# Spreading the expert gates of the first 128 tokens over the units of the U loop, from the unit at which they are known

## The chip, the cores and the metric

One core of a Trainium2 chip runs the whole program. The metric is the device time of one execution in microseconds (us), as the median of several runs. A TensorE product here is one matmul instruction with its weight load. Engines are named as the profile names them: PE is TensorE, DVE is VectorE, ACT is ScalarE, POOL is GpSimd.

## The reference, cut to what matters

The program is four layers on 256 tokens of width 1024. Two of them end in a block of many small experts (`peer`), the part that is changed. For each token eight heads each choose 16 of 16,384 experts, and the block sums over the chosen ones:

```
s = einsum('thpk,hpnk->thpn', q, sub_keys)          # two times 128 scores for each head
sv, si = top_k(s, 16)                               # level 1: the best 16 of each 128
cand = sv[:, :, 0, :, None] + sv[:, :, 1, None, :]  # level 2: the best 16 of the sums
fv, fpos = top_k(cand, 16);  gate = softmax(fv)
act = gelu(einsum('thkd,td->thk', u[eidx], x_t))
return einsum('thk,thkd->td', gate * act, v[eidx])
```

## The kernel before, in words

The kernel gathers nothing. It computes the products of all 16,384 rows of `u` with all 256 tokens, multiplies by a dense matrix of gates (zero where an expert was not chosen), and multiplies the result with all rows of `v`. So each `peer` layer has a **U loop** and a **V loop** of 128 **units** each; one unit is 128 experts. `peer` runs twice; the two are called the first and the second layer here.

One unit of the U loop takes these steps:
- a DMA brings 128 rows of `u` into a `raw` buffer (SP's queue);
- DVE transposes them in blocks, `uT` (L231), one unit further ahead than the next step;
- ACT rounds `uT` to the upper part `hi` (L159, the line of all ACT work);
- POOL forms the rest `lo = uT - hi` in four pieces of 256 columns (L261). `hi` and `lo` have two buffers each;
- PE makes 24 products (L2039): eight of `hi` with the tokens' upper part, eight of `hi` with their lower part, and, in the third pass, eight of `lo`;
- ACT applies the gelu, and the 128 x 256 result goes to the unit's slot in SBUF (`slots` for units 0 to 95, `slotb` for 96 to 127).

**Choosing the experts** goes on beside the units, as generators in `self.bgs`. `tick(1300)` (L2055) lets them go on by a fixed planned time per unit. `level1` and `level2` are almost all DVE work. They work on one half of the tokens (128) at a time, and at the end of each `level2` the count `state["have"]` goes up by 64 pairs of tokens (L1933). In the order of instructions this is at unit 29 for the first half and at unit 59 for the second.

**The gates** are made from that for two tokens at a time; there are NH = 128 such pairs, and one pair is called a gate below. `gate_ab` (L1942, DVE) marks the chosen second indices in `B`. `gates_words` (ACT, two instructions) scales by the weights into `A`. `gate_mm` (L1964, PE, four products of 128 columns) forms the gates of the pair in PSUM. For each two gates (four tokens) `gate_out` writes the result to the slots: where a unit has its gelu already, DVE multiplies the slot by the gate (L1978); where it has not, ACT copies the gate into the slot. From then on `gelu` multiplies the first `n` columns of each later unit by the gates in its slot (L2006, DVE), with a second ACT instruction for them.

Each engine runs its instructions in the order written. Within unit i that is: `gate_out` of gates whose products were made in unit i-1, `take()` (the next `hi`, `lo` and a transpose), the words of the marks made in unit i-1, the 24 products of unit i with the gate products between the second and third pass, the gelu of unit i-1, the planned share of the choosing, and last the marks `B` of the next gates. How many marks that are is what `due` says, lines L2057 to L2060.

Of the kernel before, what the change touches and what calls it, by code (L numbers as in the profile page):

```python
# [38 lines left out]
P = 128  # L39
# [78 lines left out]
class _Kernel:  # L118
# [1587 lines left out]
    def peer(self, l, after=None, result=None):  # L1706
        nc, a, T = self.nc, self.a, NX
        tc = self.tc
        with ExitStack() as st:
# [43 lines left out]
            with ExitStack() as s2:  # L1753
# [181 lines left out]
                NH = T // 2  # L1935
                ab, gps = {}, {}
                todo = {"ab": 0, "words": 0, "mm": 0, "out": 0}
# [9 lines left out]
                def gates_words():  # L1947

                    for g in range(todo["words"], todo["ab"]):
                        A = pu.tile([P, 2, P], F32, name=self.uid("A"), tag="A", bufs=4)  # L1950
                        for i in range(2):
                            self.act(A[:, i, :], ab[g][0][:, :, 0, i], "Copy", scale=gW[:, 2 * g + i:2 * g + i + 1])
                        ab[g] += (A.bitcast(F16).rearrange("p i (k n) -> p i n k", n=2),)
                    todo["words"] = todo["ab"]
# [27 lines left out]
                def gates_out():  # L1982
                    while todo["out"] * 2 + 2 <= todo["mm"]:
                        gate_out(todo["out"])
                        todo["out"] += 1

                def gates_mm(upto):
                    while todo["mm"] < upto:
                        gate_mm(todo["mm"])
                        todo["mm"] += 1  # L1990

                def gates_ab(n):
                    while n > 0 and todo["ab"] < NH:
                        gate_ab(todo["ab"])
                        todo["ab"] += 1
                        n -= 1

                def gelu(i, ps):
                    n = state["g"]
                    sl = slot(i)  # L2000
                    if n:
                        self.act(ps[:, :n], ps[:, :n], "Gelu")
                    if n < T:
                        self.act(sl[:, n:], ps[:, n:T], "Gelu")
                    if n:
                        nc.vector.tensor_mul(sl[:, :n], sl[:, :n], ps[:, :n])  # L2006
                    state["u"] = i + 1
# [20 lines left out]
                due = 0.0  # L2028
                for i in range(P):
                    gates_out()  # L2030
                    hi, lo = self.take()
                    gates = todo["words"]
                    gates_words()
                    ps = self.bank("mm")
                    for pas, (w, x) in enumerate(((hi, hh), (hi, hl), (lo, hh))):
                        if pas == 2:
                            gates_mm(gates)
                        for c in range(KC):
                            nc.tensor.matmul(ps[:, :T], w[:, c * P:(c + 1) * P], x[:, c, :],  # L2039
                                             start=(pas == 0 and c == 0), stop=(pas == 2 and c == KC - 1))  # L2040
                    if self.pend or self.follow or self.hooks:
                        self.after_unit(0.0)
                        assert i < 8
                    elif not slotb:
                        pq.close()
                        bigb = st.enter_context(tc.tile_pool(name=f"slotsb{l}", bufs=1))
                        slotb.append(bigb.tile([P, (P - NA) * NX], F32, name=f"slotb{l}"))
                    if prev is not None:
                        gelu(i - 1, prev)
                    prev = ps  # L2050
                    if i == 59:
                        assert not self.bgs
                    have = state["have"]
                    if self.bgs:
                        self.tick(1300)  # L2055
                    if have:
                        due = min(due + min((NH - todo["ab"]) / max(P - 3 - i, 1.0), 9.0 if have == NH else 0.01), 2.0)  # L2057
                        n = min(int(due), have - todo["ab"])
                        gates_ab(n)
                        due -= n  # L2060
# [224 lines left out]
```

## Time and profile before

| | us |
|---|---|
| median of 3 runs (2311.14 to 2314.92) | 2312.92 |
| the profiled execution | 2311.26 |
| its span, first to last instruction | 2309.5 |
| U loop of the first layer, span 512.56 to 941.46 | 428.90 |
| U loop of the second layer, span 1515.12 to 1943.16 | 428.04 |

The span is counted from the first instruction, and all positions below are microseconds from there. Stretches of the U loop are cut at the first of PE's 24 products of a unit. In the first layer unit 28 starts at 607.92, unit 32 at 619.36, unit 40 at 643.61, unit 44 at 657.74, unit 48 at 673.69, unit 52 at 687.07, unit 56 at 701.54, unit 60 at 713.10, unit 72 at 752.31 and unit 76 at 765.83.

How to read it: an engine that is busy for the whole of a stretch sets the pace there. Where none is, the pace is set by a chain of waits from one engine to the next.

### The profile page before, as it was taken

The page shows a single profiled execution, that of the slowest core. Times are in us where ns is not written, and L with a number is a line of the kernel's source. Part 1 is how long each engine was busy: PE and PEld are TensorE (multiplying, and loading weights), DVE is VectorE, ACT ScalarE, POOL GpSimd, SP SyncE. Part 2 cuts the span into 40 slices and gives each one's busy share as a digit, 9 for nine tenths or more (in the row PEclk, how much of TensorE's full clock was granted, in tenths as well). Part 3 has the DMA queues.
Part 4 walks back from the last instruction along what each step waited for, and adds up shares of the span by engine and source line. Part 5 has one row for each costly group of instructions (what it writes and reads, how often), then busy time and mean ns, then how long its engine had stood idle before and what let it go on. Part 6 is the DMA issues. An engine that isn't in the chain of part 4 may idle for free. (4 is left out here: it accounts for less than half of the span.)

```text
span 2309.5 us, 42025 instructions
## 1 busy us (share of the span) xinstructions
PE 2186.9 (95%) x14729; PEld 1964.3 (85%) x14729; DVE 1764.0 (76%) x3502; ACT 1291.2 (56%) x2608; POOL 1730.9 (75%) x2070
## 2 busy tenths in 40 slices
PE   8988997898999999999999988998999999999997
PEld 7768886898989999887787877998899999888886
DVE  5938888578787999678979776796969997555555
ACT  2435664554437888544444645554458886545454
POOL 1107978788999888876666685579999888777775
PEclk9999999999999999999999989999999999999999
DMA  5327755477878777577888532687878786555554
GB/s 164 110 82 235 238 172 189 134 193 149 172 154 168 156 157 155 174 254 278 306 295 306 171 110 92 195 168 150 165 159 163 156 156 155 196 196 183 200 187 141
DMA packets 285582, 414.88 MB, mean 180 GB/s; under 512 B 16489, under 2 KB 217386, under 8 KB 285370
## 3 DMA queue, kind: packets, MB, share of 16 engines
q1 hardware_dynamic: 279722, 405.30, 64.2%
q10 hardware_dynamic: 5648, 6.89, 1.1%
q8 instruction: 116, 1.90, 0.4%
q14 instruction: 96, 0.79, 0.1%
HBM read 408.98 MB, written 3.15 MB: 178 GB/s over the span
## 5 line engine op out<-in xcount | busy, mean ns | idle before, releaser
L261 POOL TENSOR_TENSOR lo<-raw,hi 128x256 fp32r<-128x256 f32 x956 | 874.9, 944 | 380.1 <-ACT hi L159 369.5
L261 POOL TENSOR_TENSOR lo<-uT,hi 128x256 fp32r<-128x256 f32 x1022 | 779.8, 801 | 80.0 <-ACT hi L159 79.5
L159 ACT ACTIVATE hi<-raw 128x1024 fp32r<-128x1024 f32 x380 | 400.7, 1057 | 422.2 <-DMA raw<-in_peer_v 200.1
L2039 PE MATMUL mm<-h,hi 128*128 128x256 f32 x4096 | 530.9, 282 | 18.8 <-ACT hi L159 17.5
L2039 PEld LDWEIGHTS mm<-h,hi 128*128 128x128 f32 x4096 | 504.4, 189 | 23.1 <-ACT hi L159 20.3
L263 DVE TENSOR_TENSOR lo<-raw,hi 128x512 fp32r<-128x512 f32 (+1 forms) x290 | 224.6, 775 | 237.1 <-ACT hi L159 236.0
L231 DVE STREAM_TRANSPOSE uT<-raw 128x1024 f32<-128x1024 f32 x256 | 316.5, 1236 | 105.1 <-POOL lo L261 78.7
L159 ACT ACTIVATE hi<-uT 128x1024 fp32r<-128x1024 f32 x256 | 271.2, 1059 | 212.0 <-DVE uT L231 196.6
L2039 PE MATMUL mm<-h,lo 128*128 128x256 f32 x2048 | 312.1, 290 | 14.2 <-POOL lo L261 11.5
L2039 PEld LDWEIGHTS mm<-h,lo 128*128 128x128 f32 x2048 | 263.8, 189 | 27.0 <-POOL lo L261 26.6
L2090 PE MATMUL mm<-hi,whi 128*128 128x512 f32 x1024 | 277.4, 392 | 4.0 <-ACT hi L159 3.6
L2090 PE MATMUL mm<-lo,whi 128*128 128x512 f32 x1024 | 275.5, 390 | 0.8 <-POOL lo L261 0.8
L2090 PE MATMUL mm<-hi,wlo 128*128 128x512 f32 x1024 | 274.7, 390 | 1.5 <-DVE wlo L494 1.5
L2090 PEld LDWEIGHTS mm<-hi,whi 128*128 128x128 f32 x1024 | 190.8, 188 | 48.0 <-ACT hi L159 6.9
L2090 PEld LDWEIGHTS mm<-lo,whi 128*128 128x128 f32 x1024 | 191.4, 188 | 43.7 <-POOL lo L261 4.2
L2090 PEld LDWEIGHTS mm<-hi,wlo 128*128 128x128 f32 x1024 | 191.9, 188 | 42.7 <-DVE wlo L494 2.7
L406 PE MATMUL mm<-h,hi 128*128 128x258 f32 (+2 forms) x1344 | 207.1, 297 | 19.8 <-ACT h L159 8.9
L406 PEld LDWEIGHTS mm<-h,hi 128*128 128x128 f32 x1344 | 181.9, 197 | 26.0 <-ACT h L159 9.9
L1942 DVE TENSOR_TENSOR B<-sin,ij 128x512 f16<-128x512 bf16 x256 | 182.8, 751 | 0.0
L159 ACT ACTIVATE A<-B,cos 128x128 f32<-128x128 f16 x512 | 167.9, 403 | 0.0
L494 DVE TENSOR_TENSOR wlo<-slots,whi 128x256 fp32r<-128x256 f32 x192 | 158.1, 824 | 0.6
L406 PE MATMUL mm<-h,lo 128*128 128x258 f32 (+2 forms) x672 | 108.8, 295 | 3.7 <-POOL lo L261 3.1
(480 smaller groups left out, 2763.7 us busy)
## 6 DMA issues: line engine op xcount, KB each, us to landing
raw<-in_peer_u SPq DMA_DIRECT2D x512, 256.0 KB
raw<-in_peer_v SPq DMA_DIRECT2D x128, 1024.0 KB
slots<-in_ada_w SPq DMA_DIRECT2D x56, 512.0 KB
scratch<-in_ada_w SPq DMA_DIRECT2D x40, 512.0 KB
raw<-in_sb_w_in SPq DMA_DIRECT2D x32, 512.0 KB
raw<-in_peer_w_q SPq DMA_DIRECT2D x32, 512.0 KB
raw<-in_od_w_in SPq DMA_DIRECT2D x24, 512.0 KB
raw<-in_ab_w_in SPq DMA_DIRECT2D x22, 512.0 KB
```

What stands on the lines that cost most here:

```text
L159: self.nc.scalar.activation(out=out, in_=in_, func=getattr(ACTF, func), **kw)
L231: self.nc.vector.transpose(ut.rearrange("p b c e -> p c b e"), src)
L261: nc.gpsimd.tensor_sub(lo[:, sl], src[:, sl], hi[:, sl].bitcast(F32))
L263: nc.vector.tensor_sub(lo[:, n:], src[:, n:], hi[:, n:].bitcast(F32))
L406: nc.tensor.matmul(ps[mm][:, :T], w[:, o:o + P], x[:, j * 4 + kk, :T], start=(j == 0 and n_of[mm] == 1), stop=(j == nu - 1 and n_of[mm] == ...
L494: nc.vector.tensor_sub(lo, src, hi.bitcast(F32))
L1942: nc.vector.tensor_tensor(out=B.rearrange("p j n i -> p j (n i)"), in0=iota4, in1=ij[:, g].rearrange("p n i -> p (n i)").unsqueeze(1).to_b ...
L2039: nc.tensor.matmul(ps[:, :T], w[:, c * P:(c + 1) * P], x[:, c, :], start=(pas == 0 and c == 0), stop=(pas == 2 and c == KC - 1))
L2090: nc.tensor.matmul(outs[t][d], w[:, t * P:(t + 1) * P], v[:, 512 * d:512 * d + 512], start=(i == 0 and pas == 0), stop=(i == P - 1 and pas ...
```

## The change

One line is changed. `due` is the number of gates owed; each unit adds to it the gates left to make, over the units left up to three before the end.

```diff
                     if have:
-                        due = min(due + min((NH - todo["ab"]) / max(P - 3 - i, 1.0), 9.0 if have == NH else 0.01), 2.0)
+                        due = min(due + (NH - todo["ab"]) / max(P - 3 - i, 1.0), 2.0)
                         n = min(int(due), have - todo["ab"])
                         gates_ab(n)
                         due -= n
```

Before, the added amount was held to 0.01 while only the first half of the tokens was known, so the first mark stood at unit 59, and from unit 67 on each unit made two. Now marks stand from unit 29 on, in the pattern 1, 1, 2. The total stays at 128 gates in each layer. Whatever stands behind a gate moves with it: two ACT words, four PE products, and the write to the slots. Since gates now come earlier, more of `gate_out` is ACT copies and less DVE products, and more units have gated columns in their gelu.

DVE, unit 41 of the first layer, from where the choosing for the second half of the tokens goes on (`slots` holds its scores and indices) to the transpose of unit 42. Before:

```order
L1738 MATCH_REPLACE slots_4220<-slots_4220 128x54 x2
L1741 MAX slots_4220<-slots_4220 128x8 x2
L1744 MAX_INDEX slots_4220<-slots_4220 128x8 x2
L1875 COPY slots_4220<-slots_4220 128x8
L1876 TENSOR_TENSOR slots_4220<-slots_4220 128x8x15
L1877 CAST slots_4220<-slots_4220 128x128
L1882 TENSOR_SCALAR slots_4220<-slots_4220 128x128 x8
L1884 TENSOR_SCALAR slots_4220<-slots_4220 128x128
L231 STREAM_TRANSPOSE uT_6863<-raw_70 128x4x8x32
```

The same place now:

```order
L2006 TENSOR_TENSOR slots_4220<-slots_4220,mm_6919 128x24
L1738 MATCH_REPLACE slots_4220<-slots_4220 128x54 x2
L1741 MAX slots_4220<-slots_4220 128x8 x2
L1744 MAX_INDEX slots_4220<-slots_4220 128x8 x2
L1875 COPY slots_4220<-slots_4220 128x8
L1876 TENSOR_TENSOR slots_4220<-slots_4220 128x8x15
L1877 CAST slots_4220<-slots_4220 128x128
L1882 TENSOR_SCALAR slots_4220<-slots_4220 128x128 x8
L1884 TENSOR_SCALAR slots_4220<-slots_4220 128x128
L1942 TENSOR_TENSOR B_7031<-sin_90,ij 128x512
L1978 SCALAR_TENSOR_TENSOR slots_4220<-aux_6936,slots_4220 128x41x4
L231 STREAM_TRANSPOSE uT_7047<-raw_70 128x4x8x32
```

The choosing stands at the same unit as before; the transpose now stands behind a gelu's product, a mark and a `gate_out` product as well (in every third unit two marks and no `gate_out`). From unit 29 to unit 58, 40 marks, 18 `gate_out` products (of 128 to 228 columns) and 26 gelu products (of 4 to 72 columns) are added on DVE in this way; 16, 8 and 11 of them in units 32 to 43. A mark of unit i has its products on PE in unit i+2, so 38 gates have theirs before unit 60.

ACT, late in the U loop of the first layer, one unit and the start of the next (`A` are the words of a gate; each has four products on PE). Before:

```order
L159 ACTIVATE hi_10059<-uT_10007 128x1024
L159 ACTIVATE A_10072<-B_10052,cos_89 128x128 x2
L159 ACTIVATE A_10075<-B_10054,cos_89 128x128 x2
L159 ACTIVATE mm_10015<-mm_10015 128x156
L159 ACTIVATE slotb_5212<-mm_10015 128x100
L159 ACTIVATE slotb_5212<-s_10095 128x26x4
L159 ACTIVATE hi_10122<-uT_10070 128x1024
```

Now, where as many tokens have their gates:

```order
L159 ACTIVATE hi_9648<-uT_9603 128x1024
L159 ACTIVATE A_9661<-B_9643,cos_89 128x128 x2
L159 ACTIVATE mm_9611<-mm_9611 128x156
L159 ACTIVATE slots_4220<-mm_9611 128x100
L159 ACTIVATE slots_4220<-s_9681 128x6x4
L159 ACTIVATE slotb_5212<-s_9681 128x32x4
L159 ACTIVATE hi_9706<-uT_9659 128x1024
```

In place of two gates in each late unit there is one in two units of three and two in the third.

## Rows read from the trace of the kernel before

**Rows 1.** Page, part 1: busy us (share of the span) x instructions
```profile
span 2309.5 us, 42025 instructions
PE 2186.9 (95%) x14729; PEld 1964.3 (85%) x14729; DVE 1764.0 (76%) x3502; ACT 1291.2 (56%) x2608; POOL 1730.9 (75%) x2070
```
**Rows 2.** Stretches, first layer: units 28-31, 32-39, 40-43, 44-47, 48-51, 52-55, 56-59, 28-59
```profile
core 0: us, PE busy (x) PEld busy (x) DVE busy (x) ACT busy (x) POOL busy (x), PEclk, DMA share, GB/s
607.92:619.36 11.44, 11.44 (x99) 11.44 (x98) 10.00 (x39) 5.33 (x8) 11.13 (x16) 1.00 0.98 187
619.36:643.61 24.25, 23.75 (x195) 22.99 (x194) 22.45 (x94) 10.65 (x16) 22.28 (x33) 1.00 0.86 169
643.61:657.74 14.13, 11.67 (x99) 11.37 (x97) 13.50 (x64) 5.13 (x8) 10.83 (x16) 0.99 0.83 171
657.74:673.69 15.95, 14.43 (x97) 13.19 (x98) 11.37 (x11) 5.53 (x9) 15.95 (x17) 0.90 0.67 133
673.69:687.07 13.38, 12.37 (x99) 11.55 (x98) 8.77 (x10) 5.33 (x8) 13.38 (x17) 1.00 0.78 156
687.07:701.54 14.47, 12.56 (x99) 11.64 (x97) 9.35 (x15) 8.09 (x11) 12.31 (x17) 1.00 0.75 148
701.54:713.10 11.56, 11.56 (x102) 11.56 (x101) 6.29 (x9) 5.33 (x8) 11.49 (x18) 1.00 0.85 168
607.92:713.10 105.18, 97.77 (x775) 93.75 (x774) 81.74 (x235) 45.38 (x67) 97.36 (x129) 0.98 0.81 161
```
**Rows 3.** Waits of DVE in units 28-39, then in units 44-55
```profile
DVE uT L231 <- DMA raw<-in_peer_u: 2.5, 2, 1.3
...
DVE uT L231 <- POOL lo L261: 14.2, 11, 3.1
```
**Rows 4.** Groups of ACT, units 28-59: busy, mean ns | idle before, releasers
```profile
L159 ACT ACTIVATE hi<-uT 128x1024 fp32r<-128x1024 f32 x32 | 33.9, 1060 | 56.5 <-DVE uT L231 54.4 <-DVE slots L1732 2.1
```
**Rows 5.** Stretches, first layer: units 72-75, 112-115, 60-127
```profile
752.31:765.83 13.52, 13.52 (x130) 13.36 (x130) 12.95 (x21) 12.03 (x37) 12.30 (x17) 1.00 0.76 157
887.78:901.35 13.57, 13.57 (x130) 13.41 (x129) 13.57 (x25) 11.30 (x33) 12.13 (x17) 1.00 0.80 156
713.10:941.46 228.36, 228.36 (x2146) 225.71 (x2145) 212.34 (x356) 192.29 (x555) 207.94 (x276) 1.00 0.78 159
```
**Rows 6.** Gate products on PE (L1964 alone), units 72-75
```profile
752.31:765.83 13.52, 2.66 (x32) 2.02 (x32) 1.00 0.76 157
```
**Rows 7.** The marks, line L1942: duration ns min/median/max
```profile
L1942 DVE TENSOR_TENSOR B<-sin,ij x256: 376/690/972, 713.5 to 1932.9; 128x512 f16<-128x512 bf16 x128
```
**Rows 8.** The marks alone, units 60-71
```profile
713.10:752.31 39.21, 13.36 (x22) 1.00 0.84 168
```
**Rows 9.** Groups by shape on DVE, units 60-127
```profile
L1978 DVE SCALAR_TENSOR_TENSOR slots<-aux,slots 128x244 f32<-128x244 f32 x1 | 0.4, 396 | 0.0
L1978 DVE SCALAR_TENSOR_TENSOR slotb<-s,slotb 128x120 f32<-128x120 f32 x1 | 0.3, 272 | 0.0
L2006 DVE TENSOR_TENSOR slots<-slots,mm 128x68 f32<-128x68 f32 x1 | 0.2, 224 | 0.2 <-ACT slots L159 0.2
L2006 DVE TENSOR_TENSOR slots<-slots,mm 128x4 f32<-128x4 f32 x2 | 0.2, 119 | 0.0
```
**Rows 10.** Stretches, second layer: units 28-59, 32-43, 60-127
```profile
1610.23:1714.52 104.29, 96.31 (x774) 92.21 (x773) 82.28 (x235) 45.37 (x67) 97.14 (x129) 1.00 0.81 163
1621.62:1659.38 37.76, 34.96 (x291) 34.20 (x289) 36.27 (x157) 15.78 (x24) 33.26 (x49) 1.00 0.85 173
1714.52:1943.16 228.64, 228.64 (x2147) 225.96 (x2146) 212.30 (x356) 192.11 (x555) 207.76 (x275) 1.00 0.79 158
```
**Rows 11.** Groups of POOL, units 28-31, units 44-47, units 72-75
```profile
L261 POOL TENSOR_TENSOR lo<-uT,hi 128x256 fp32r<-128x256 f32 x16 | 11.3, 739 | 0.3 <-ACT hi L159 0.3
...
L261 POOL TENSOR_TENSOR lo<-uT,hi 128x256 fp32r<-128x256 f32 x17 | 16.2, 994 | 3.0 <-ACT hi L159 3.0
...
L261 POOL TENSOR_TENSOR lo<-uT,hi 128x256 fp32r<-128x256 f32 x17 | 13.0, 802 | 1.2 <-ACT hi L159 1.1
```
**Rows 12.** Stretches before, in and behind a fall of the granted clock
```profile
652.00:657.70 5.70, 3.25 (x27) 3.05 (x26) 5.56 (x17) 1.09 (x2) 2.70 (x4) 0.99 0.75 174
...
657.70:661.10 3.40, 3.38 (x16) 3.38 (x17) 2.55 (x3) 1.57 (x3) 3.36 (x4) 0.52 0.22 74
661.10:664.52 3.42, 3.42 (x30) 3.30 (x29) 2.44 (x2) 1.33 (x2) 3.42 (x4) 1.00 1.14 204
```

## The prediction

> **What bounds the kernel now.** I read the page's busy shares first [rows 1]: PE is busy for 95% of the span, DVE and POOL for 75 to 76%. That is an average over unlike stages, so I cut the U loop into stretches of four to eight units next. They show two regimes.
>
> Late in the loop, from unit 60 to the end, PE is busy for 228.36 of 228.36 us [rows 5]. Four units with two gates each take 13.52 us there (3.38 a unit), and 13.57 us forty units later. DVE goes from 12.95 busy to 13.57 of 13.57 between these two rows and the pace does not follow it: PE sets it. The 32 products of eight gates can be seen in the row for L1964 alone [rows 6].
>
> In the middle, units 28 to 59, no gate is made and nothing is full throughout: of 105.18 us PE is busy for 97.77, POOL for 97.36, DVE for 81.74 [rows 2]. Units 28 to 31 are PE's pace without gates, 11.44 us of 11.44, 2.86 a unit. Units 32 to 43 belong to DVE, which chooses the experts of the second half: 35.95 of 38.38 us. ACT waits 54.4 us for the transpose in units 28 to 59 [rows 4], so what delays DVE is passed to ACT, POOL and PE. In units 44 to 51 POOL is full, 29.33 of 29.33 us, and DVE has 20.14 us of work; its idle time in units 44 to 55 is a wait of 14.2 us for POOL to release buffers [rows 3].
>
> So the change takes work from a stretch that PE paces to one where DVE, POOL and PE in turn set the pace.
>
> **What is taken away: late units.** A late gate costs PE the difference of two paces: (13.52 - 11.44) us / 8 gates = 0.26 us [rows 2, 5]. By the order, 38 gates of a layer have their products before unit 60 now. From unit 60 on PE is therefore relieved of 38 x 0.26 = 9.9 us a layer. The next engine there leaves room: with 1.33 gates a unit DVE loses a third of its marks, POOL has 12.30 of 13.52 us, ACT 12.03 [rows 5], and PE's new pace is 2.86 + 1.33 x 0.26 = 3.21 us a unit, 12.83 for four. I take the whole 9.9 us.
>
> **What is added: DVE in units 29 to 58.** A mark takes 0.376 us at its shortest and 0.972 at its longest [rows 7]; the 22 marks of units 60 to 71, where POOL is nearly full as in the middle, cover 13.36 us, 0.607 each [rows 8]. I take 0.607. A `gate_out` product of 120 columns takes 0.272 us and one of 244 takes 0.396 [rows 9], so those of 128 to 228 columns are near 0.33, and near 0.30 in units 32 to 43. A gelu product takes 0.119 us for 4 columns and 0.224 for 68 [rows 9], on average 0.155, and 0.14 in units 32 to 43. The sum is 40 x 0.607 + 18 x 0.33 + 26 x 0.155 = 24.3 + 5.9 + 4.0 = 34.2 us a layer. DVE's idle time in units 28 to 59 is 105.18 - 81.74 = 23.4 us [rows 2], so even a perfect packing leaves 10.8 us over. By stretch, for the first layer:
> - Units 32 to 43: 16 x 0.607 + 8 x 0.30 + 11 x 0.14 = 13.6 us more on DVE, into 38.38 - 35.95 = 2.4 us of idle time: +11.2 us. The four marks of units 29 to 31 (2.4 us) find 11.44 - 10.00 = 1.4 us: +1.0.
> - Units 44 to 51: 11 marks, 5 and 8 products are 9.8 us; DVE goes to 30.0 us against 29.33, and POOL grows as well. Its subtraction takes 0.739 us beside no mark and 0.802 beside two a unit [rows 11], so one mark costs POOL 4 x 0.063 / 2 = 0.13 us, 1.4 us for 11. Two engines, each full and each waiting for the other, lose more than the larger of these: I take +3, between 0.7 and the whole 9.8.
> - Units 52 to 55: 4.9 us onto 9.35 of 14.47: +0.5, for the order in which it comes.
> - Units 56 to 59: PE's own pace with gates, 12.83 against 11.56: +1.3.
>
> That is 17.0 us. In the second layer the same DVE work meets 37.76 - 36.27 = 1.5 us of idle time in units 32 to 43 in place of 2.4 [rows 10]: 17.7 us or so. Its late part is as the first layer's, 228.64 us of PE.
>
> **Edits at nothing.** The added ACT work in the middle (two words of a gate, copies, a second gelu instruction) is at most what late units do, 12.03 us in 13.52 [rows 5], where units 32 to 39 use 10.65 of 24.25 [rows 2]. If that cover were gone, `hi` would be late by the same amount. PE's added gate products, 9.9 us, fill its waits in units 32 to 55, which the terms above lengthen. No DMA and no instruction of SP's or POOL's queue is moved past another. The V loop is untouched.
>
> **Sum.** 17.0 - 9.9 = +7.1 us in the first layer and 17.7 - 9.9 = +7.8 in the second, +14.9 together. On the profiled execution's own 2311.26 us (span 2309.5) that is 2326; the median shown, 2312.92, lies 1.7 above, so I predict 2328 us.
>
> **A rule weighed.** Two engines share a way into SBUF here, and the row puts the price of a mark for POOL at 0.13 us [rows 11]. The Trainium skill, "SBUF — State Buffer", section "Who interferes with whom", says that a VectorE instruction with two SBUF inputs contends with a GpSimd instruction that reads SBUF, and that the one that starts second is blocked until the other has ended. By that rule a mark would cost POOL its whole length, not 0.13 us; the late units, with two marks each, do not show it, though the marks' own lengths, from 0.376 to 0.972 us [rows 7], agree with one engine held up by the other. What it would make of the time is the third rival.
>
> **The rivals.**
> 1. Faster: the marks only fill waits and PE's work alone counts. For it: DVE idles 23.4 us in the middle and PE 7.4. PE would then need 97.77 + 9.9 = 107.7 us for units 28 to 59 in place of 105.18, +2.5, and each layer gains 7.4: 2311 - 15 = 2296, 2298 by the median. It needs DVE's lead over PE, two units of buffers, to outlast units 32 to 43. Against it: there DVE has 13.6 us more for 2.4 us of room, and the lead is used up already where PE waits, 11.67 busy of 14.13 us in units 40 to 43 [rows 2]. It decides once the added DVE work in units 32 to 43 fits their 2.4 us of room; with the shortest marks it is still 16 x 0.376 + 3.9 = 9.9. Chance 0.08.
> 2. No change: all marks at 0.376 us. Then units 28 to 43 pay 20 x 0.376 + 3.9 - 3.9 = 7.5 us, units 56 to 59 1.3, the rest nothing, and 8.8 stands against 9.9: 2309, 2311 by the median. For it: POOL is less than full while DVE paces, and marks beside an idle POOL may be short. Against it: POOL is not idle for long, 22.28 of 24.25 us in units 32 to 39 [rows 2]. Chance 0.10.
> 3. POOL is blocked for a mark's whole length. Full POOL in units 44 to 51 then pays 11 x 0.607 = 6.7 us and not 1.4, some 5 us a layer: 2338 by the median. For it: beside the long choosing instructions of units 44 to 47 a subtraction takes 0.994 us and not 0.739 [rows 11]. Chance 0.12.
> 4. Nothing is hidden: every added DVE instruction lengthens the units, since `gate_out` and gelu products now make DVE wait for PE, where it ran ahead. 34.2 - 9.9 = 24.3 us a layer: 2361 by the median. Against it: products of the gates are two units old and DVE has shown no wait for PE in these units [rows 3]. Chance 0.06.
>
> That the change does not do what it says is excluded: the order shows the 40 marks.
>
> PE's clock can add a little to all of these. Before units 44 to 47, PE was busy for 3.25 of 5.70 us, and the granted clock then fell to 0.52 for 3.40 us, which is the level of 1.2 GHz; PE made 16 products in it and 30 in the next 3.42 us at 1.00 [rows 12]. More starving of PE may bring more such stretches, each worth up to 1.7 us; where DVE sets the pace they are hidden. I leave them out of the sum and keep them in the upper end.
>
> **How the numbers follow.** The forecast has the rest, 0.64; its own range is 2318 to 2340 (the units 44 to 51 between 0.7 and 6 us a layer, marks between 0.5 and 0.7). A measurement of this kernel can tell about 0.2%, 4.6 us, from no change, so the bounds are 2308.3 and 2317.5. Faster: rival 1 and a little of rival 2, 0.10. Within: most of rival 2 and the lower edge of the forecast, 0.10. Slower: 0.80. The range from 2311 to 2346 holds the forecast, rival 3 and half of rival 2; rivals 1 and 4 lie outside.
>
> **What would show it.** Units 32 to 43 at 49 to 51 us in place of 38, with DVE full and PE starved: if they stay under 43, the middle is wrong. Late units at 3.2 us with PE still full: if they stay at 3.38, the gain is not there, and if DVE or POOL is full in them, PE was not alone. Marks in the middle near 0.6 us. Units 44 to 51 above 31 us, and POOL's subtractions there near 1.0 us or longer. If the whole is not slower, the added DVE work must have found more idle time than 23.4 us, or have become shorter than 0.6 us a mark.

## The result and the profile after

The changed kernel takes 2330.9 us, median of 4 runs (2328.75 to 2337.51), against 2312.03 us for 4 runs of the kernel before: a ratio of 1.0097, 95% interval 1.0073 to 1.0121. It is slower, by 18.9 us by the medians; 15 were forecast. The profiled execution took 2330.08 us against 2311.26.

The page's first part, as in [rows 1], shows almost nothing of this:

```profile
span 2328.3 us, 42061 instructions
PE 2197.2 (94%) x14729; PEld 1973.4 (85%) x14729; DVE 1761.2 (76%) x3540; ACT 1312.7 (56%) x2686; POOL 1746.7 (75%) x2070
```

No share moves by more than a point, since the work is nearly the same and mostly its place is another. The stretches show it. These are, of the first layer after, units 28-31, 32-43, 44-51, 52-55, 56-59, then units 72-75, 60-127 and 28-59; the columns are those of [rows 2]:

```profile
611.45:623.32 11.87, 11.87 (x104) 11.79 (x102) 10.30 (x41) 6.05 (x10) 11.22 (x16) 1.00 0.99 190
623.32:673.60 50.28, 44.37 (x354) 41.79 (x352) 48.39 (x191) 31.42 (x83) 35.76 (x48) 0.93 0.65 129
673.60:705.13 31.53, 28.52 (x237) 26.33 (x238) 30.33 (x40) 20.91 (x56) 30.15 (x33) 1.00 0.68 134
705.13:722.16 17.03, 14.22 (x119) 13.03 (x117) 13.96 (x29) 12.97 (x32) 12.39 (x17) 1.00 0.65 126
722.16:735.35 13.19, 13.19 (x122) 13.02 (x120) 12.11 (x22) 10.75 (x30) 12.48 (x18) 1.00 0.76 157
774.15:787.23 13.08, 13.08 (x123) 12.92 (x121) 10.11 (x17) 9.92 (x29) 12.65 (x17) 1.00 0.83 164
735.35:954.92 219.57, 219.57 (x1994) 216.86 (x1993) 177.39 (x291) 165.97 (x455) 210.70 (x275) 1.00 0.80 164
611.45:735.35 123.90, 112.17 (x927) 105.96 (x925) 115.09 (x319) 82.09 (x208) 101.99 (x129) 0.97 0.70 139
```

Units 32 to 43 go from 38.38 us [rows 2, its second and third row] to 50.28, with DVE busy for 48.39. The late units go from 228.36 [rows 5] to 219.57, still PE's from end to end. The second layer repeats both; its units 28-59, 32-43, 52-55 and 60-127 answer to [rows 10]:

```profile
1620.10:1742.68 122.58, 110.97 (x927) 104.64 (x924) 115.48 (x318) 81.96 (x210) 101.60 (x128) 0.99 0.69 138
1631.86:1680.98 49.12, 43.33 (x354) 40.58 (x352) 47.25 (x191) 30.79 (x81) 34.72 (x46) 0.97 0.64 129
1712.50:1729.50 17.00, 14.20 (x118) 13.01 (x117) 13.94 (x29) 12.96 (x32) 12.38 (x17) 1.00 0.61 126
1742.68:1961.97 219.29, 219.29 (x1994) 216.56 (x1993) 178.87 (x291) 165.15 (x452) 209.97 (x275) 1.00 0.80 164
```

Units 28 to 59 lose 18.7 and 18.2 us, the late units return 8.8 and 9.4: +18.8 together, the whole difference of the two profiled executions. (The second layer's unit 28 before is taken at its first product, 1610.15; the row in [rows 10] starts 0.08 us later.) Units 0 to 27, whose order is the same, took 2.9 us longer in this profile and the rest of the program 2.9 less. Over the profiles with that order (the two kernels and experiments 1 to 4 and 9) units 0 to 27 lie between 95.0 and 97.4 us a layer, so this is the runs' own variation.

What DVE was given, units 28-59 of the first layer, in groups:

```profile
L1942 DVE TENSOR_TENSOR B<-sin,ij 128x512 f16<-128x512 bf16 x40 | 27.8, 713 | 0.0
L2006 DVE TENSOR_TENSOR slots<-slots,mm 128x8 f32<-128x8 f32 (+17 forms) x26 | 4.4, 171 | 5.1 <-ACT slots L159 4.4
L1978 DVE SCALAR_TENSOR_TENSOR slots<-s,slots 128x132 f32<-128x132 f32 (+8 forms) x9 | 3.0, 336 | 0.3 <-ACT slotb L159 0.3
L1978 DVE SCALAR_TENSOR_TENSOR slots<-aux,slots 128x128 f32<-128x128 f32 (+8 forms) x9 | 3.0, 330 | 0.3 <-ACT slotb L159 0.3
```

The busy times of these groups add up to 38.2 us, where 34.2 was forecast: the marks are longer, 27.8 us for 40, 0.69 each, where the forecast took 0.607 by the same measure. But DVE's busy time in the stretch rises only by 115.09 - 81.74 = 33.4 us. Records of neighbours on the engine overlap at their ends: all its groups here add up to 131.2 us for 115.09 busy, and before to 91.6 for 81.74, so the overlap grew with the work. The two errors cancel. And ACT's waits in the same units:

```profile
ACT A L159 <- DVE B L1942: 26.6, 28, 3.4
ACT hi L159 <- DVE uT L231: 7.8, 11, 2.4
ACT slots L159 <- DVE slots L1890: 2.8, 1, 2.8
ACT slots L159 <- DVE slots L1884: 2.7, 1, 2.7
```

Before, ACT waited 54.4 us for the transposition [rows 4]. Now it waits for marks, with `hi` queued behind its copies of them. The engine that is late is the same one.

### The profile page after: what moved, and what is told of

Same layout as the page of the kernel before. It is cut to its first block, busy times and chain, and to the rows that moved or that the text cites. A ratio compares the mean times of both kernels' runs of the same rounds, so it can differ in the third digit from the quotient of the medians.

```text
span 2328.3 us, 42061 instructions
## 1 busy us (share of the span) xinstructions
PE 2197.2 (94%) x14729; PEld 1973.4 (85%) x14729; DVE 1761.2 (76%) x3540; ACT 1312.7 (56%) x2686; POOL 1746.7 (75%) x2070
## 5 line engine op out<-in xcount | busy, mean ns | idle before, releaser
L261 POOL TENSOR_TENSOR lo<-uT,hi 128x256 fp32r<-128x256 f32 x1022 | 794.1, 814 | 86.9 <-ACT hi L159 83.3
L2039 PE MATMUL mm<-h,lo 128*128 128x256 f32 x2048 | 316.6, 293 | 12.1 <-POOL lo L261 10.3
L159 ACT ACTIVATE A<-B,cos 128x128 f32<-128x128 f16 x512 | 175.7, 402 | 53.5 <-DVE B L1942 53.5
L1942 DVE TENSOR_TENSOR B<-sin,ij 128x512 f16<-128x512 bf16 x256 | 175.2, 704 | 0.0
```

The costliest lines, as they stand in the source:

```text
L159: self.nc.scalar.activation(out=out, in_=in_, func=getattr(ACTF, func), **kw)
L261: nc.gpsimd.tensor_sub(lo[:, sl], src[:, sl], hi[:, sl].bitcast(F32))
L1942: nc.vector.tensor_tensor(out=B.rearrange("p j n i -> p j (n i)"), in0=iota4, in1=ij[:, g].rearrange("p n i -> p (n i)").unsqueeze(1).to_b ...
```

## The experiments

Pairs of values below are first layer / second layer. Runs with an interval have several rounds; the others are one profiled run, read by their stretches.

**1. Gates only from unit 44.** The changed kernel, with nothing made in the stretch that DVE paces:

```
-                    if have:
+                    if have and i >= 44:
```

> The changed kernel, but the gates of the first half are held until unit 44, so that the stretch that DVE fills (units 32 to 43) has no marks. If DVE's work there is the price: units 32 to 43 take 38 us again (50 in the changed kernel), units 44 to 59 some 6 to 8 us more than in the kernel before (23 gates), the late units 5 to 6 us less, so 0 to +2 us a layer and 2312 to 2318 us. If each gate before unit 60 costs the same wherever it stands (18.5 us for 40, 0.46 each): +11 and -5.5 a layer, 2323 us.

2314.9 us against 2310.26, ratio 1.002 (1.0001 to 1.004). Its units 32-43, 52-55 and 60-127:

```profile
620.37:658.12 37.75, 34.74 (x290) 33.94 (x288) 35.89 (x156) 15.75 (x24) 33.19 (x48) 0.99 0.87 173
688.46:706.80 18.34, 15.56 (x123) 14.66 (x121) 15.28 (x30) 13.88 (x34) 13.55 (x18) 0.91 0.64 123
720.19:943.58 223.39, 223.39 (x2062) 220.67 (x2061) 193.40 (x322) 176.10 (x497) 209.05 (x275) 1.00 0.79 161
```

Units 32-43 are back at 37.75 / 37.18 us: the 12 us a layer are paid for gates made there. But units 52-55 become 18.34 / 18.47, longer than in either kernel, and keep this version from gaining. Part of that may be PE's clock: the granted clock fell once inside these units in both layers (0.91 is the mean of the stretch), and did not in either layer of the two kernels.

**2. Marks alone.** The kernel before, with 16 marks more in units 32 to 43 that nothing reads:

```
+                    if 32 <= i < 44:
+                        for _ in range(2 if i % 3 == 1 else 1):
+                            spare_mark()
```

> The kernel before, with 16 marks that nobody reads added on DVE in units 32 to 43 of each layer; no words, no products, no writes to the slots. If DVE's time sets the pace there: 16 x 0.61 - 2.4 = 7 to 8 us more in these units (45 to 46 us in place of 38.4), nothing elsewhere, 2325 to 2328 us in all. If the price of the changed kernel comes from the gates' PE products, ACT words or copies: under 2 us in these units.

Units 32-43:

```profile
620.30:664.11 43.81, 37.99 (x290) 36.14 (x288) 43.14 (x169) 15.74 (x24) 35.22 (x47) 0.96 0.77 149
620.30:664.11 43.81, 0.00 (x0) 0.00 (x0) 7.97 (x13) 0.00 (x0) 0.96 0.77 149
```

43.81 / 43.94 us, +5.4 / +6.2 where 7 to 8 was expected: DVE is full (43.14). The second line, of the marks alone, says why it is less: only 13 of the 16 ran before unit 44 began (14 in the second layer). Their 7.97 us less the 2.4 us of idle time is 5.5, what was measured; in the second layer 8.76 less 1.5 is 7.3, for a measured 6.2. In the changed kernel 16 marks run in these units, and marks alone make about half of its +11.9. What brought the rest, the gate and gelu products (3.9 us in the forecast), the three marks more or the waits around them, no run separates.

**3. Products alone.** The kernel before, with the gates' work on PE in the middle and none of DVE's: 4 spare 128x128 products a unit (8 in every third) in units 31 to 59.

```
+                    if 31 <= i < 60:
+                        for k in range(8 if i % 3 == 0 else 4):
+                            nc.tensor.matmul(ps[:, T + k % 2 * P:T + (k % 2 + 1) * P], spare[:, :P], spare[:, :P],
```

> The kernel before, with 4 or 8 products of 128 columns added on PE at the end of each of units 31 to 59 (as many as the changed kernel has gate products there), nothing on other engines. If PE's added work hides in its waits there: units 28 to 59 take 105 to 109 us (105.2 before). If PE's time counts in full: 115 us.

Units 28-59:

```profile
612.77:719.78 107.01, 104.27 (x926) 100.73 (x925) 83.00 (x237) 46.41 (x68) 99.77 (x132) 1.00 0.83 162
```

107.01 / 106.37 us, +1.8 / +2.0, while PE's busy time grows by 6.5: PE's part is mostly hidden in its waits, as the prediction had it. Units 32-43 take 38.82 / 38.32 us of it, +0.4 / +0.6.

**4. Products put back late.** The changed kernel, with 152 spare products (38 gates' worth) in the late units that lost a gate:

```
+                    if i >= 61:
+                        for k in range(4 * lack[i]):
+                            nc.tensor.matmul(ps[:, T + k % 2 * P:T + (k % 2 + 1) * P], spare[:, :P], spare[:, :P],
```

> The changed kernel, with 4 products of 128 columns added in late units, 152 in each layer, so that PE has as much work from unit 60 on as in the kernel before; DVE, ACT and POOL keep the changed kernel's lighter load. If PE sets the pace of the late units: units 60 to 127 take 227 to 229 us (228.4 before, 219.5 in the changed kernel). If DVE's marks set it: 219 to 221 us.

Units 60-127:

```profile
729.20:959.72 230.52, 230.52 (x2147) 226.24 (x2145) 178.31 (x290) 164.61 (x450) 209.21 (x274) 1.00 0.75 156
```

230.52 / 230.54 us, a little above the 227 to 229 expected: PE's products alone take the whole gain away again, with DVE's and ACT's relief left in place. PE sets the late pace.

**5. Without the gates' exponential.** The stretch that surprised was units 52-55. There ACT loads a table, takes the exponential of the second half's gates and loads the old table again. The changed kernel with a constant in place of the exponential, so that neither load is needed (the exponential is left out):

```
-                    self.act(gt3, gt3, "Exp")
+                    self.act(gt3, gt3, "Identity", scale=0.0, bias=self.ones[:, :1])
```

> The changed kernel without the exponential of the gates: an ACT instruction that writes ones stands in its place, so the two table loads around it are gone, and its wait for DVE's last sum (L1912) stays. If units 52 to 55 are long (17.0 us in place of 14.5 before) because the gelu, and with it DVE's gelu product, waits behind the two table loads of 1.28 us each and the exponential: 14.5 to 15.5 us. If DVE's own added work is the reason: 16.5 to 17.1.

Units 52-55:

```profile
705.68:721.28 15.60, 13.59 (x118) 12.80 (x117) 14.00 (x30) 10.90 (x31) 14.78 (x17) 1.00 0.68 134
```

15.60 / 16.04 us in place of 17.03 / 17.00, between the two expectations. Without the loads these units are 1.4 / 1.0 us shorter, and DVE's longest wait for a gelu falls from 2.60 to 0.6 us. The kernel before has the same two loads, and no run takes them out there; so how much of the +2.6 / +2.8 they make is not shown.

**6. The exponential one unit later.** In the kernel before, ACT loads the table and then waits 3.46 us for the subtraction ahead of the exponential (the first two lines), with `hi` of the next unit behind it:

```profile
689.39 1.28 ACT L153 ACT_TABLE_LOAD   x1
694.13 0.31 ACT L159 ACTIVATE slots<-slots 128x128 f32<-128x128 f32 x1 [3.46 <-DVE slots L1912]
694.34 1.04 ACT L159 ACTIVATE hi<-uT 128x1024 fp32r<-128x1024 f32 x1
```

So the kernel before with the exponential issued later than the subtraction:

```
                     nc.vector.tensor_sub(gt3, fv3, fv3[:, :, 0:1].to_broadcast([P, 8, 16]))
+                    yield 1300.0
                     self.act(gt3, gt3, "Exp")
-                    yield 2000.0
+                    yield 700.0
```

> The kernel before, with the exponential written one unit later than DVE's sum that it waits for; nothing is left out. If the wait of ACT for that sum (3.5 us in units 52 to 55) holds back the upper parts behind it: units 52 to 55 take 12.3 to 13 us in place of 14.5, 1.5 to 2.2 us a layer, with a little more in units 20 to 25, 2306 us or a ratio of 0.997 to 0.9985 in all. If POOL or PE fills these units anyway: no change.

2305.01 us against 2309.45, 5 rounds, ratio 0.9977 (0.996 to 0.9994). Units 52-55 and the same instructions:

```profile
686.38:699.35 12.97, 12.37 (x98) 11.65 (x97) 10.06 (x15) 8.21 (x11) 12.58 (x17) 1.00 0.71 142
...
691.90 1.28 ACT L153 ACT_TABLE_LOAD   x1
693.69 0.31 ACT L159 ACTIVATE slots<-slots 128x128 f32<-128x128 f32 x1 [0.51 <-DVE slots L1912]
```

12.97 / 13.70 us in place of 14.47 / 14.19; the wait is 0.51. This beats both kernels, by 0.2% the one before. The two stretches are 2.0 of the 4.4 us; in units 20 to 27, where the exponential of the first half stands, this profile is 0.1 us longer and 1.2 us shorter than the one before, and where the rest comes from is open.

**7 and 8. The same edit beside the added gates:** on experiment 1, and on the changed kernel.

> First-half gates from unit 44 on as in the run from_44, and the exponential one unit later. There, units 52 to 55 took 18.4 us and units 44 to 51 30.3, against 5 us less in the late units. If the wait for the exponential is what the gates meet in units 52 to 55: these take 14 to 15.5 us, and the whole is 3 to 4 us a layer below the run from_44: 2306 us, a ratio near 0.998. If DVE's added work is: 2313 to 2315.

> The changed kernel with the exponential one unit later. The stretch that DVE fills is as in the changed kernel: units 32 to 43 stay at 49 to 51 us. If the wait for the exponential is the price in units 52 to 55: 14 to 15 us there in place of 17.0, 2323 to 2326 in all. If not: 17 us and 2330.

On experiment 1: 2310.21 us, ratio 1.0005 (0.9991 to 1.0019), units 52-55 18.23 / 20.31. On the changed kernel: 2328.9, units 52-55 16.40 / 17.17. Both missed what was expected of the wait, 14 to 15.5 and 14 to 15: with gates in these units the exponential's wait is not the main thing that makes them long. A load then stands ahead of a gelu, and DVE's gelu product waits for that, 2.5 us and 1.9 us in the first layers. The granted clock fell inside these units in both layers of the first of the two (mean 0.91 and 0.92) and in the second layer of the other (0.90); the 16.40, with no fall, is the cleanest of the four.

**9 and 10. The gelu product one unit later,** so that DVE doesn't stand at it while ACT is late: on the changed kernel, and on experiment 7.

```
+                    gated()
                     if n:
-                        nc.vector.tensor_mul(sl[:, :n], sl[:, :n], ps[:, :n])
+                        wait.append((sl[:, :n], ps[:, :n]))
```

> The changed kernel with each gelu product of DVE (L2006) written one unit later, behind the next unit's; nothing is left out, and the exponential stays where it was. If units 52 to 55 are long because DVE, in order, waits 2.6 us for a gelu that stands behind the table loads: 15 to 16 us in place of 17.0, and units 32 to 43 as they were (49 to 51). If DVE's added work alone makes them long: 16.8 to 17.3.

> First-half gates from unit 44, the exponential one unit later, and the gelu product one unit later. With the wait for the gelu gone from DVE: units 52 to 55 at 14.5 to 16 us (18.2 to 20.3 without the last step), units 56 to 59 at 13.4 and the late units 5 us below the kernel before: 2302 to 2306 us, ratio 0.996 to 0.998. If the marks themselves fill these units: 18 us there, and 2310 us, ratio 1.000.

On the changed kernel 2320.76 us in one run: units 32-43 48.77 / 48.49, 44-51 30.81 / 30.84, but units 52-55 still 17.24 / 17.37. DVE's wait there has only moved, to the gate product:

```profile
DVE slots L1978 <- ACT slotb L159: 2.4, 1, 2.4
```

On experiment 7: 2309.21 against 2309.33, ratio 0.9997 (0.9981 to 1.0014), units 52-55 17.16 / 16.09. That is below experiment 7's 18.23 / 20.31, but the clock fell there and here not. So DVE's place in the queue for that one product is not the whole cause either; that whatever needs ACT first waits is argued from these waits, not shown.

**11. No gates in units 52 to 55.** Experiment 10 with gates in 44-51 and from 56:

```
+                    if have and (44 <= i < 52 or i >= 56):
```

> As the run from_44_exp_mul_later, but with no marks in units 52 to 55. Some 12 gates are then made in units 44 to 51. If it is the marks and what they bring that lengthen units 52 to 55: 13 to 14 us there, and with 1 us more in units 44 to 51 and 2.5 us less in the late units 2302 to 2305 us, ratio 0.996 to 0.998. If the gelu products beside the table loads do: 15 us or more there and no better than the run before_exp_later (0.9977).

2303.56 us against 2309.33, 5 rounds, ratio 0.9974 (0.9959 to 0.9989): it beats the kernel before, and is not to be told apart from experiment 6. Units 52-55 and 60-127:

```profile
687.01:702.02 15.01, 14.10 (x111) 12.73 (x109) 13.37 (x26) 12.36 (x29) 13.32 (x17) 1.00 0.66 126
714.64:939.33 224.69, 224.69 (x2086) 221.94 (x2085) 196.23 (x337) 180.65 (x515) 209.29 (x275) 1.00 0.78 161
```

Units 52-55 fall by 2.1 / 1.6 us against experiment 10. Against the kernel before, 44-51 cost +1.0 / +1.0, and the late units give back 3.7 / 3.8. But this kernel has experiment 6's later exponential in it. Against experiment 6, which moves no gate, 44-51 cost 1.0 / 1.0, units 52-55 2.0 / 0.8 and 56-59 0.9 / 1.1, and the late units return 3.2 / 3.2: the moved gates pay back what they cost, and no gain of theirs can be told.

## Why the prediction was right, and where its sizes were off

The mechanism held, in both signs: work was taken off PE where PE sets the pace, and more was lost where DVE does. By its own terms, forecast and then measured, first / second layer:

| units | forecast | measured |
|---|---|---|
| 28-31 | +1.0 | +0.4 / +0.3 |
| 32-43 | +11.2 / +11.9 | +11.9 / +11.4 |
| 44-51 | +3 | +2.2 / +2.2 |
| 52-55 | +0.5 | +2.6 / +2.8 |
| 56-59 | +1.3 | +1.6 / +1.5 |
| 60-127 | -9.9 | -8.8 / -9.4 |
| both layers | +14.9 | +18.8 |

Three of its counts are a little off, without weight for the forecast. The second layer's +11.9 is what its 17.7 leaves; its own 13.6 - 1.5 gives 12.1. By the pattern 1, 1, 2 from unit 29, units 44 to 51 hold 10 marks and not 11, and units 52 to 55 hold 6. And 11, 5 and 8 instructions at its prices are 9.6 us, not 9.8. Its +3 for units 44 to 51 was chosen between 0.7 and 9.8, so that it came near is partly luck.

**DVE in units 32-43.** Right in place, cause and size: experiment 1 takes the whole of it away, experiment 2 brings about half of it with marks only, experiment 3 shows that PE's share is small. The marks there took 10.02 us for 16, 0.626 each, where 0.607 was taken:

```profile
623.32:673.60 50.28, 10.02 (x16) 0.93 0.65 129
```

The sum also got there without a wait that it didn't know of: two copies of gates on ACT wait 2.8 and 2.7 us for choosing instructions (L1890 and L1884 in the waits above); both sides work in the tile `slots`, which is presumably why. DVE was full meanwhile, so this adds little; that last point is argued, since no run took that wait away.

**Units 52-55, the step that failed.** The prediction put +0.5 "for the order in which it comes" and set the added ACT work at nothing, by a sum over stretches in which ACT had room. Here ACT had two table loads and a wait that such a sum doesn't hold. After, in units 52-55 (start us, us, instruction, idle before it in brackets; the last line is DVE's):

```profile
713.13 0.31 ACT L159 ACTIVATE slots<-slots 128x128 f32<-128x128 f32 x1 [1.47 <-DVE slots L1912]
713.34 1.04 ACT L159 ACTIVATE hi<-uT 128x1024 fp32r<-128x1024 f32 x1
714.29 1.31 ACT L159 ACTIVATE A<-B,cos 128x128 f32<-128x128 f16 x4
715.62 1.28 ACT L153 ACT_TABLE_LOAD   x1
716.91 0.20 ACT L159 ACTIVATE mm<-mm 128x56 f32<-128x56 f32 x1
717.14 0.34 ACT L159 ACTIVATE slots<-mm 128x200 f32<-128x200 f32 x1
...
717.52 0.21 DVE L2006 TENSOR_TENSOR slots<-slots,mm 128x56 f32<-128x56 f32 x1 [2.60 <-ACT slots L159]
```

From 713.13 on ACT stands still no more, and DVE's product of the gelu waits 2.60 us for it: the load stands between. In the late units before, from which the zero was taken, DVE's product of the gelu waited for ACT 13 times, 0.7 us at the longest. What makes the excess is shown in part: making gates there at all is worth 2.1 / 1.6 us (experiment 11 against 10), and taking the loads out 1.4 / 1.0 (experiment 5), though what that would save in the kernel before was not measured. The two overlap. How it divides between the copies of marks, the gelus' second instruction, the loads and DVE's order is open: experiments 7 to 10 each moved one of them, and none brought these units back to 14 or 15 us. The Trainium skill, "ScalarE: Activation LUTs", section "What ACT_TABLE_LOAD costs", gives 1283 ns for the load and a drain of about 1380 ns with it. The trace agrees on the load, 1.28 us; behind this one the next instruction starts 0.01 us after its end, so a drain is not seen at that place.

**The late units.** The 38 gates returned 0.23 / 0.25 us each and not 0.26. Experiment 4 leaves PE as the engine that paces them, so rival 1's half of the argument was right there; in the middle, where it needed DVE's lead to last, it failed as priced.

**POOL and rival 3.** Its subtractions in units 44-47 and 48-51 after:

```profile
L261 POOL TENSOR_TENSOR lo<-uT,hi 128x256 fp32r<-128x256 f32 x17 | 17.0, 1037 | 2.3 <-ACT hi L159 2.3
...
L261 POOL TENSOR_TENSOR lo<-uT,hi 128x256 fp32r<-128x256 f32 x17 | 15.1, 927 | 1.4 <-ACT hi L159 1.4
```

The first was 994 [rows 11]; the second, before:

```profile
L261 POOL TENSOR_TENSOR lo<-uT,hi 128x256 fp32r<-128x256 f32 x17 | 14.1, 870 | 0.0
```

Together that is 17 x 0.043 + 17 x 0.057 = 1.7 us for the 10 marks that ran there, 0.17 each. The prediction's 0.13 nearly held and the mark's whole length did not: by the Trainium skill's rule ("SBUF — State Buffer", "Who interferes with whom"), as the prediction read it, 10 marks of 0.607 us would have cost POOL an estimated 6.1 us. Rival 2 is out, since the marks averaged 0.69 us; rival 4 is out, since the middle paid 18.5 us a layer for 33.4 us of DVE work.

## What to carry to other kernels

Idle time summed over a stage is no room: 23.4 us of it took in 33.4 us of work at a price of 18.5 us a layer. Cut the stage at the places where the pacing engine changes, and price the move piece by piece. In a piece with a rare instruction in an engine's queue (a table load, a wait for another stage), don't carry over "this work is hidden" from pieces that lack it. Look at such queues before moving work at all: one `yield` set elsewhere took 0.2% off the kernel, and the best placing of the gates, which has that `yield` in it too, took off no more that can be told. That a piece where the moved work's own engine has room is the right place is argued here, not shown: in experiment 11 units 44-51 cost 1.0 us more than in experiment 6, and units 52-59, to which later steps of the same gates and new gates fall, 3.0 / 1.9.

## What the runs showed of the hardware that was not expected

PE's granted clock fell more often with PE starved in the middle: twice in units 32-43 of the first layer after, for about 3.4 us each, and once in those of the second; before, once as unit 44 of the first layer began [rows 12] and not in the second. Ahead of the second fall and in it:

```profile
664.50:669.40 4.90, 1.55 (x13) 1.35 (x13) 4.02 (x25) 2.51 (x7) 1.06 (x2) 1.00 0.92 185
669.47:672.88 3.41, 3.41 (x20) 3.32 (x19) 3.00 (x8) 0.79 (x3) 1.86 (x3) 0.51 0.24 39
```

PE was busy for 1.55 of 4.90 us, and then the clock stood at the level of 1.2 GHz. DVE was 88% busy during the fall and paced these units, so that the prediction's choice to leave the falls out cost little is likely; no run takes the falls away.

A mark's length went with POOL's work beside it. Two pairs of marks, then POOL's subtractions around them:

```profile
689.92 1.83 DVE L1942 TENSOR_TENSOR B<-sin,ij 128x512 f16<-128x512 bf16 x2
713.01 0.75 DVE L1942 TENSOR_TENSOR B<-sin,ij 128x512 f16<-128x512 bf16 x2
689.41 2.94 POOL L261 TENSOR_TENSOR lo<-uT,hi 128x256 fp32r<-128x256 f32 x3
714.46 2.13 POOL L261 TENSOR_TENSOR lo<-uT,hi 128x256 fp32r<-128x256 f32 x3 [2.44 <-ACT hi L159]
```

The first pair runs while POOL works and takes 1.83 us; the second runs while POOL waits and takes 0.75. Over units 44-51, where POOL is busy for 30.15 of 31.53 us, ten marks cover 8.76 us; over units 52-55, where it is busy for 12.39 of 17.03, six cover 3.50. So rival 2's "for" held, marks beside an idle POOL are short, and its "against" decided: POOL was rarely idle.
